# A whole transformer step on one core: FFN tiles from unnormed rows, row broadcasts by diagonals, a moved branch, idle products

## The chip, the core and the metric

The kernel runs on one core of a Trainium2 chip. The metric is device time in microseconds (us) of one execution. TensorE is called PE, VectorE DVE, ScalarE ACT, GpSimd POOL, SyncE SP; SP issues the weight transfers. A *pass* is one matmul of the trace; a row of the order of instructions (below) can stand for several.

## The reference

256 tokens of 1024 numbers go through one block (retention and gated delta rule, then a mixture of 32 experts of which each token takes two) and then through a pooling mixer and a convolutional FFN. What the change touches is this:

```python
    # router: top-1 group, top-2 experts in it; then, over the tokens of each expert,
    hid = silu(xs @ w1[e]) * (xs @ w3[e]);  ys = (hid @ w2[e]) * gate
    x = x + gate2 * ffn
    x = rmsnorm(x, final_norm_w)                       # a row of 1024 weights
    # pooling mixer: x + scale * (pool(rms_norm(x, norm_mix_g)) @ w + b)
    # FFN:
    h = causal_depthwise_conv(rms_norm(x, norm_ffn_g) @ w_in, conv_w, conv_b)   # 1024 -> 5632, 3 taps
    val, gate = split(h, 2)
    out = x + (silu(gate) * val) @ w_out               # 2816 -> 1024
```

## The kernel before, in words

The kernel is one long program without loops on the chip. The front (projections, retention, delta rule) takes until about 232 us, the router until about 240, the experts until 682, the pooling mixer until 708, the FFN until the end.

**Experts.** The loop over `p` (0 to 15) takes two experts each, 64 slots per expert in each half of the 128 rows. For one p PE does w1 and w3 (L1268: 64 passes of 128x512), then ACT the silu (L1273), DVE the product `hid` (L1274), PE the scatter of the pair before (L1226), transposes of `hid` (L1279), at odd p the gather of the tokens of the next two pairs (L1203), then `slot_rows` (L1213, L1215) and w2 (L1291: 32 passes). Six weight blocks of 2 MB per pair come by SP's queue into a ring of slots: a block is asked for when the products that read the slot's old content are done. For p = 15 each block comes in four pieces. At p = 12 `load_tail` closes one part of the ring, leaves six slots, and makes three broadcast rows: it loads 1x3072 numbers by DMA, and six matmuls with a contraction of 1 (L1039) spread them over 128 rows.

**Overflow.** An expert with more than 64 tokens is handled by `overflow()` (L1153), a `tc.If` on a count in SBUF. Every engine loads the count (L1154) and branches (L1155). The body is not run for these inputs. The call stands between the first gather and w1 of p = 0.

**Tail.** `pw` is multiplied by the scale row `psb` on POOL (L1334). The statistics of both norms run on ACT and DVE, L1372 is the pooling product, `zs` its evacuation (L1376, L1378), L1388 the banded product, and four adds make the new rows x (L1391, one for each half of the two token tiles t = 0, 1). Then come squares (L1392), root and reciprocal (L1394 to L1396), the scaled rows `v` (L1399), their transposes (L1414), and two parts of each transposed row block: the rounded `gh` (ACT, L1419) and the rest `gl` (DVE, L1422).

**FFN.** `up(j)` (j = 0 to 10) makes four products of 24 passes (L288: three parts, eight blocks each). Before a product its weights are split into `wh` (ACT, L279) and `wl` (DVE or POOL, L282). After it ACT applies the last tap (L1443) and DVE two shifted taps (L1446, `yf`), then silu (L1449), a product on POOL (L1450) and a split into `hfh` and `hfl`. Four PSUM banks take turns.

Inside the experts the order of PE and SP is that of the code (`tc.manual_schedule`), in the router that of DVE. A scheduler orders the rest.

Of the kernel before, what the change touches and what calls it, by code (L numbers as in the profile page):

```python
# [9 lines left out]
F32 = mybir.dt.float32  # L10
F32R = mybir.dt.float32r
# [8 lines left out]
D = 1024  # L20
# [39 lines left out]
def _consts():  # L60
# [38 lines left out]
    def pack(d):  # L99
        off, cols, n = {}, [], 0  # L100
        for k, v in d.items():
# [10 lines left out]
         ("bge", 40), ("fnT", 8), ("mixgT", 8), ("ffngT", 8), ("fconvw", 132), ("fconvb", 44)]  # L112
# [8 lines left out]
def layout(inp):  # L121
# [56 lines left out]
def build(ctx, tc, io, out, dbg=None):  # L178
# [842 lines left out]
    def load_tail():  # L1021
        ringd.close()
        rings["c"] = ctx.enter_context(tc.tile_pool(name="ringc", bufs=RING_C, reuse_waits="tile"))
        slots[:] = [s for s in slots if s[0] in "efh"] + [["c", None] for i in range(RING_C)]
        tail_w["split"] = ctx.enter_context(tc.tile_pool(name="ffnw", bufs=1, reuse_waits="tile"))
        tlw = tlws.enter_context(tc.tile_pool(name="tailw", bufs=1, reuse_waits="tile"))

        def tw(shape, name):
            return tlw.tile(shape, F32, name=name)

        cp = tw([128, CP.shape[1]], "cp")
        pw = tw([128, 4, 2, 256], "pw")
        rows = tw([128, 3, D], "rows")
        rf = rows.rearrange("p i d -> p (i d)")
# [7 lines left out]
        tail_w.update(cp=cp, pw=pw, fwb=fwb, pbb=rows[:, 1, :], psb=psb)  # L1042
# [17 lines left out]
    hand.enter_context(tc.manual_schedule(engines={ENG.DVE}))  # L1060
# [49 lines left out]
    V.tensor_tensor(M, oh[0], oh[1], op=ALU.add)  # L1110
    psk = bank("pa")
# [41 lines left out]
    def overflow():  # L1153
            nmax = nc.values_load(bigi[0:1, 0:1], min_val=0, max_val=T)  # L1154
            with tc.If(nmax > SLOTS):  # L1155
# [13 lines left out]
                with tc.For_i(0, NE, 1) as e:  # L1169
                    gcol = sr([128, 2], "gcol")  # L1170
                    V.tensor_copy(gcol, gov[:, :, bass.ds(e, 1)].rearrange("p t o -> p (t o)"))
                    for f in range(4):
                        hps = [bank(), bank()]
                        for i, nm in enumerate(("w1", "w3")):
                            for k4 in range(0, 8, 4):
                                wb = mt([128, 4, 128], "wb", tag="hid")
# [67 lines left out]
    overflow()  # L1244
    for p in range(NE // 2):
# [18 lines left out]
        for nm in ("w1", "w3"):  # L1264
# [117 lines left out]
    w0 = wload(io["ffn_w_in"][0], 8, 512)  # L1382
    for t in range(2):
        for hf in range(2):
# [7 lines left out]
            S.activation(junk, x1[:, t, cs], AF.Square, accum_out=s5[:, t, hf:hf + 1])  # L1392
        r5 = s5[:, t, 1:2]
        V.tensor_scalar(s5[:, t, 0:1], s5[:, t, 0:1], 1.0 / D, EPS, op0=ALU.mult, op1=ALU.add)  # L1394
        S.activation(r5, r5, AF.Sqrt, scale=1.0 / D, bias=s5[:, t, 0:1])
        V.reciprocal(r5, r5)  # L1396
        for hf in range(2):
            cs = slice(512 * hf, 512 * hf + 512)
            V.tensor_scalar(v3[:, t, cs], x1[:, t, cs], r5, None, op0=ALU.mult)  # L1399
    dump("x4", x1)  # L1400
    for i in range(2):
        for vg in range(2):
            c = 256 * vg + 128 * i
            pre.append(split(tail_w["split"], w0[:, :, c:c + 128], [128, 8, 128], "w", NSPLIT))

    gh, gl = [], []
# [3 lines left out]
    for k2 in range(4):  # L1410
        ps = bank("pa").rearrange("p (k t) -> p k t", k=2)
        for t in range(2):
            for k in range(2):
                PE.transpose(ps[:, k, 128 * t:128 * t + 128], v3[:, t, 128 * (2 * k2 + k):128 * (2 * k2 + k) + 128], ident)  # L1414
        h = ff.tile([128, 2, T], F32R, name="gh", tag="gh", bufs=4)
        l = ff.tile([128, 2, T], F32R, name="gl", tag="gl", bufs=4)
        for k in range(2):
            g = ffng[:, 2 * k2 + k:2 * k2 + k + 1]
            S.activation(h[:, k, :], ps[:, k, :], AF.Copy, scale=g)  # L1419
        for k in range(2):  # L1420
            g = ffng[:, 2 * k2 + k:2 * k2 + k + 1]
            V.scalar_tensor_tensor(l[:, k, :], ps[:, k, :], g, h.bitcast(F32)[:, k, :], op0=ALU.mult, op1=ALU.subtract)  # L1422
            gh.append(h[:, k, :])
            gl.append(l[:, k, :])
# [6 lines left out]
    def up(j):  # L1431
        w = wload(io["ffn_w_in"][j], 8, 512) if j else None
        for i in range(2):
            ys = []
            for vg in range(2):
                m = 22 * vg + 2 * j + i
                c = 256 * vg + 128 * i
                wh, wl = split(tail_w["split"], w[:, :, c:c + 128], [128, 8, 128], "w", NSPLIT) if j else pre.pop(0)
                ps = bank()
                for k in range(8):  # L1440
                    mm3(ps[:, :T], wh[:, k, :], wl[:, k, :], gh[k], gl[k], k == 0, k == 7)
                y = ff.tile([128, T], F32, name="yf", tag="yf", bufs=4)
                S.activation(y, ps[:, :T], AF.Identity, scale=cw[:, 3 * m + 2:3 * m + 3], bias=cb[:, m:m + 1])  # L1443
                for tap in range(2):
                    sh = 2 - tap
                    V.scalar_tensor_tensor(y[:, sh:], ps[:, :T - sh], cw[:, 3 * m + tap:3 * m + tap + 1], y[:, sh:],  # L1446
                                           op0=ALU.mult, op1=ALU.add)
                ys.append(y)
            S.activation(ys[1], ys[1], AF.Silu)  # L1449
            G.tensor_tensor(ys[0], ys[0], ys[1], op=ALU.mult)  # L1450
            hid_parts[2 * j + i] = split(ff, ys[0], [128, T], "hf", 8)
# [39 lines left out]
```

## Time and profile before

| | |
|---|---|
| three runs | 893.80, 897.24, 897.35 us; median 897.24 |
| profiled execution | 895.82 us; span 894.0 us, mean granted clock 0.978 |
| busy PE / DVE / ACT / POOL | 843.3 / 387.0 / 271.0 / 147.0 us |
| DMA | 288.52 MB, mean 323 GB/s over the span |
| L1268 and L1291 on PE | 229.0 and 115.4 us |
| L288 on PE | the three FFN forms 97.9, 97.7 and 97.7 us |

PE is busy for 94% of the span, so time can only go where PE waits, or where it does work that can be left out. From 280 to 710 us the DMA engines are full as well. A row of a timeline gives the start, the length, the engine and the line; "[2.12 <-DVEq L1155]" says that the engine had been idle for 2.12 us, and what let it go on. "PEldq", "ACTq" are the engines' sequencers.

### The profile page before, as it was taken

The page shows a single profiled execution, that of the slowest core. Times are in us where ns is not written, and L with a number is a line of the kernel's source. Part 1 is how long each engine was busy: PE and PEld are TensorE (multiplying, and loading weights), DVE is VectorE, ACT ScalarE, POOL GpSimd, SP SyncE. Part 2 cuts the span into 40 slices and gives each one's busy share as a digit, 9 for nine tenths or more (in the row PEclk, how much of TensorE's full clock was granted, in tenths as well). Part 3 has the DMA queues.
Part 4 walks back from the last instruction along what each step waited for, and adds up shares of the span by engine and source line. Part 5 has one row for each costly group of instructions (what it writes and reads, how often), then busy time and mean ns, then how long its engine had stood idle before and what let it go on. Part 6 is the DMA issues. An engine that isn't in the chain of part 4 may idle for free.

```text
span 894.0 us, 12890 instructions
## 1 busy us (share of the span) xinstructions
PE 843.3 (94%) x5326; PEld 532.7 (60%) x5326; DVE 387.0 (43%) x708; ACT 271.0 (30%) x505; POOL 147.0 (16%) x107
## 2 busy tenths in 40 slices
PE   3988999989889999999999998999998899999998
PEld 0665788767733434343343433434434799999996
DVE  2477587586511222221122211322115776566564
ACT  2244144364410101010010100201003575555652
POOL 0244331162000000000000000000002024523525
PEclk9899999999999999999999999899999999999999
DMA  9982679767579999999999999999999935454001
GB/s 372 423 358 98 284 263 378 290 254 321 189 264 403 427 427 428 427 427 427 427 426 427 429 427 427 427 385 429 421 409 425 426 122 221 154 229 186 1 2 47
DMA packets 26112, 288.52 MB, mean 323 GB/s; under 512 B 3009, under 2 KB 3393, under 8 KB 9793
## 3 DMA queue, kind: packets, MB, share of 16 engines
q1 hardware_dynamic: 26050, 287.66, 78.3%
q8 instruction: 43, 0.70, 0.3%
q14 instruction: 19, 0.16, 0.0%
HBM read 286.60 MB, written 1.05 MB: 322 GB/s over the span
## 4 chain that ended last, share of the span: by engine, by line
PE 59%; DMA 9%; DVE 2%; issue 1%; ACT 1%; SPq 0%; ACTq 0%
PE ps L288 20%; PE ps L1268 19%; PE ps L1291 11%; DMA wt<-in_w 9%; PE ps L1226 3%; PE ps L1203 3%; PE ps L1279 1%; PE ps L1039 1%; PE ps L1215 1%; DVE wl L282 0%; PE ps L1213 0%; DVE x L1474 0%; DVE x L1391 0%; PE ps L1362 0%; ACT gh L1419 0%
## 5 line engine op out<-in xcount | busy, mean ns | idle before, releaser
L1268 PE MATMUL ps<-wt,x 128*64 128x512 f32 x1024 | 229.0, 600 | 5.4 <-DMA wt<-in_w 3.2
L1268 PEld LDWEIGHTS ps<-wt,x 128*64 128x64 f32 x1024 | 76.2, 138 | 150.8 <-issue 137.8
L279 ACT ACTIVATE wh<-wt 128x512 fp32r<-128x512 f32 (+1 forms) x138 | 114.1, 833 | 92.8 <-PE ps L288 84.4
L1291 PE MATMUL ps<-wt,hidT 128*64 128x512 f32 x512 | 115.4, 599 | 2.7 <-issue 1.9
L282 POOL TENSOR_TENSOR wl<-wt,wh 128x512 fp32r<-128x512 f32 (+1 forms) x52 | 96.0, 1857 | 86.6 <-ACT wh L279 84.1
L282 DVE TENSOR_TENSOR wl<-wt,wh 128x1024 fp32r<-128x1024 f32 (+1 forms) x86 | 84.0, 986 | 43.0 <-ACT wh L279 42.5
L1274 DVE SCALAR_TENSOR_TENSOR hid<-ps,gs,hid 128x512 f32<-128x512 f32 x16 | 12.0, 750 | 203.6 <-PE ps L1268 203.6
L288 PE MATMUL ps<-gh,wh 128*128 128x256 f32 x352 | 97.9, 279 | 1.4 <-ACT gh L1419 1.4
L288 PE MATMUL ps<-gl,wh 128*128 128x256 f32 x352 | 97.7, 278 | 0.0
L288 PE MATMUL ps<-gh,wl 128*128 128x256 f32 x352 | 97.7, 278 | 0.0
L1334 POOL TENSOR_TENSOR pw<-pw,rows 128x512 f32<-128x512 f32 x4 | 5.0, 1270 | 467.5 <-DVE Yf L1298 467.5
L1291 PEld LDWEIGHTS ps<-wt,hidT 128*64 128x64 f32 x512 | 39.2, 138 | 65.7 <-issue 63.0
L288 PEld LDWEIGHTS ps<-gh,wh 128*128 128x128 f32 x352 | 66.7, 190 | 1.8 <-ACT gh L1419 1.6
L288 PEld LDWEIGHTS ps<-gl,wh 128*128 128x128 f32 x352 | 66.8, 190 | 0.2
L288 PEld LDWEIGHTS ps<-gh,wl 128*128 128x128 f32 x352 | 66.7, 189 | 0.0
L1302 ACT ACTIVATE Yh<-ps 128x512 fp32r<-128x512 f32 x30 | 17.9, 597 | 108.3 <-DVE ps L1300 63.6
L1446 DVE SCALAR_TENSOR_TENSOR yf<-ps,sm,yf 128x254 f32<-128x254 f32 x88 | 41.7, 479 | 12.3 <-ACT yf L1443 10.8
L1300 DVE TENSOR_TENSOR ps<-ps,g2b 128x512 f32<-128x512 f32 x30 | 21.0, 699 | 59.9 <-PE ps L1291 59.9
L1273 ACT ACTIVATE hid<-ps 128x512 f32<-128x512 f32 x16 | 9.6, 597 | 110.3 <-PE ps L1268 110.3
L215 ACT ACTIVATE x<-ps,modT,A 128x256 f32<-128x256 f32 x32 | 17.8, 565 | 77.4 <-PE ps L1203 77.4
L1450 POOL TENSOR_TENSOR yf<-yf 128x256 f32<-128x256 f32 x22 | 19.7, 894 | 99.3 <-ACT yf L1449 66.0
L380 PE MATMUL ps<-wt,srep 128*32 128x512 f32 x160 | 24.5, 751 | 11.8 <-DMA wt<-in_w_ada 11.8
(376 smaller groups left out, 1253.1 us busy)
## 6 DMA issues: line engine op xcount, KB each, us to landing
wt<-in_w SPq DMA_DIRECT2D x86, 2048.0 KB, 21.6
wt<-in_w_ada SPq DMA_DIRECT2D x12, 2048.0 KB, 14.0
wt<-in_ffn_w_in SPq DMA_DIRECT2D x11, 2048.0 KB, 12.2
wt<-in_w SPq DMA_DIRECT2D x40, 512.0 KB, 10.2
wt<-in_w_in SPq DMA_DIRECT2D x7, 2048.0 KB, 14.1
wt<-in_ffn_w_out SPq DMA_DIRECT2D x5, 2048.0 KB, 7.6
wt<-in_w_out SPq DMA_DIRECT2D x2, 2048.0 KB, 8.1
wt<-in_w_in SPq DMA_DIRECT2D x2, 1024.0 KB, 19.5
```

Of the source, the lines that this page charges most:

```text
L279: S.activation(hi, src, AF.Copy)
L282: (eng or V).tensor_tensor(lo, src, hi.bitcast(F32), op=ALU.subtract)
L288: PE.matmul(ps, lhsT=a, rhs=b, start=first and n == 0, stop=last and n == 2)
L380: PE.matmul(ps[32 * q:32 * q + 32, :], lhsT=srep[:, 2 * q + kk, :], rhs=w[:, 2 * q + kk, :], start=kk == 0, stop=kk == 1)
L1203: PE.matmul(ps[d - d % 2][:, d % 2, :], lhsT=x[:, t, 128 * d:128 * d + 128], rhs=OH[:, t].rearrange("p g s -> p (g s)"), start=t == d % 2 ...
L1226: PE.matmul(res[t, c], lhsT=oT[:, 128 * t:128 * t + 128], rhs=y, start=False, stop=False)
L1268: PE.matmul(ps[64 * g:64 * g + 64, :], lhsT=xg[:, k, 128 * (p % 2) + 64 * g:128 * (p % 2) + 64 * g + 64], rhs=wt[p, nm, g][:, k, :], start ...
L1291: PE.matmul(py[c][64 * g:64 * g + 64, :], lhsT=hidT[:, f, 64 * g:64 * g + 64], rhs=wt[p, "w2", g][:, f, 512 * c:512 * c + 512], start=f == ...
L1300: V.tensor_tensor(py[c], py[c], g2c, op=ALU.mult)
L1302: S.activation(yh, py[c], AF.Copy)
L1446: V.scalar_tensor_tensor(y[:, sh:], ps[:, :T - sh], cw[:, 3 * m + tap:3 * m + tap + 1], y[:, sh:], op0=ALU.mult, op1=ALU.add)
L1450: G.tensor_tensor(ys[0], ys[0], ys[1], op=ALU.mult)
```

## The change

There are five edits.

1. `spin()` puts five 128x128 matmuls into the router, whose results nobody reads: three before the ranks, two after the counts. PE's order in the router is now that of the code.
2. `overflow()` is called behind the w1 products of p = 0. The silu follows w1 at once for every p.
3. The three broadcast rows are made at p = 13, behind the scatter: POOL makes diagonals (128x512, two buffers), and PE multiplies them with a matrix of ones over the full contraction. The row DMA is gone.
4. `pw` is no longer scaled; `zs` takes the scale row in its evacuation, all four on DVE. The transposed rows of t = 1 are evacuated by ACT in eight pieces.
5. The FFN starts with the unscaled rows x: tiles j = 0, 1 use `gh0` and `gl0` from x, and DVE multiplies the eight products in PSUM by the row of reciprocal norms `r5`. `norm_row()` makes `r5` after the second product. The scaled rows `v`, their 16 transposes and `gh`, `gl` for j of 2 and more are made during j = 1.

```diff
+    def spin(n):
+        ps = bank("pa")
+        for i in range(n):
+            PE.matmul(ps[:, :128], lhsT=ident, rhs=ident, start=True, stop=True)
...
-        nc.sync.dma_start(rf[0:1, :], io["rows"])
-        V.tensor_tensor(rows[0:1, 1, :], rows[0:1, 1, :], rows[0:1, 2, :], op=ALU.mult)
-        for i in range(6):
-            ps = bank("pa")
-            PE.matmul(ps, lhsT=cav("ones")[0:1, :], rhs=rf[0:1, 512 * i:512 * i + 512], start=True, stop=True)
-            copy(rf[:, 512 * i:512 * i + 512], ps)
...
+    def tail_rows():
+        bp = tail_w["pool"].tile([128, 8], F32, name="bp", tag="bp")
+        V.tensor_tensor(bp, smv("pbT"), smv("psT"), op=ALU.mult)
+        for i, col in enumerate((smv("fnT"), bp, smv("psT"))):
+            for hf in range(2):
+                dg = tail_w["pool"].tile([128, 4, 128], F32, name="dg", tag="dg", bufs=2)
+                G.tensor_tensor(dg, ident[:, None, :].to_broadcast([128, 4, 128]),
+                                col[:, 4 * hf:4 * hf + 4, None].to_broadcast([128, 4, 128]), op=ALU.mult)
+                ps = bank("pa")
+                PE.matmul(ps, lhsT=cav("ones"), rhs=dg.rearrange("p b c -> p (b c)"), start=True, stop=True)
+                copy(tail_w["rows"][:, i, 512 * hf:512 * hf + 512], ps)
...
     gather(0, OH)
-    overflow()
     for p in range(NE // 2):
...
+            if nm == "w1":
+                hid = mt([128, DE], "hid")
+                S.activation(hid, ps, AF.Silu)
+                if not p:
+                    overflow()
...
         if p:
             scatter(*prev, 1)
+        if p == 13:
+            tail_rows()
...
-    for g in range(4):
-        G.tensor_tensor(pw[:, g], pw[:, g], psb[:, None, 256 * g:256 * g + 256].to_broadcast([128, 2, 256]), op=ALU.mult)
...
+            V.scalar_tensor_tensor(zs[:, t, cs], ps, s4[:, t, 1:2], psb[:, cs], op0=ALU.mult, op1=ALU.mult)
...
+    rows_T(x1, gh0, gl0)
...
+    def norm_row():
+        psr = bank("pa")
         for t in range(2):
+            for hf in range(2):
+                S.activation(junk, x1[:, t, 512 * hf:512 * hf + 512], AF.Square, accum_out=s5[:, t, hf:hf + 1])
...
+            V.tensor_scalar(dg, ident, r, None, op0=ALU.mult)
+            PE.matmul(psr[:, 128 * t:128 * t + 128], lhsT=cav("ones"), rhs=dg, start=True, stop=True)
+            V.tensor_scalar(v3[:, t], x1[:, t], r, None, op0=ALU.mult)
+        S.activation(r5, psr[:, :T], AF.Copy)
...
+        ahead = [product(*m) for m in tiles[:0 if j else 2]]
+        if not j:
+            norm_row()
...
+            if j < 2:
+                V.tensor_tensor(ps[:, :T], ps[:, :T], r5, op=ALU.mult)
...
+            if i and j == 1:
+                rows_T(v3, gh, gl, (2 * vg, 2 * vg + 1))
```

PE at the start of the experts, before (`xh`, `xl`: rows of all tokens; `wt`: a weight block; the body of the branch is left out):

```order
L1203 MATMUL ps<-OH,xh 128x256 x16
L1203 MATMUL ps<-OH,xl 128x256 x16
L1154 TENSOR_LOAD router
L1155 COMPARE_AND_BRANCH
...
L1155 UNCONDITIONAL_BRANCH x2
L1268 MATMUL ps<-wt,x_73 64x512 x32
```

and after, where lines have moved by 14 or 15 numbers:

```order
L1083 MATMUL ps<-ca 128x128 x2
L1218 MATMUL ps<-OH,xh 128x256 x16
L1218 MATMUL ps<-OH,xl 128x256 x16
L1282 MATMUL ps<-wt,x_73 64x512 x16
L1169 TENSOR_LOAD router
L1170 COMPARE_AND_BRANCH
...
L1170 UNCONDITIONAL_BRANCH x2
L1282 MATMUL ps<-wt,x_73 64x512 x16
```

Half of the 32 rows (the w1 products) now stands ahead of the branch, the w3 half behind it, and two idle products ahead of the gather.

PE at the broadcast rows, before, behind the scatter of p = 11 and ahead of w1 of p = 12:

```order
L1226 MATMUL ps<-Yh,oT 128x512
L1226 MATMUL ps<-Yl,oT 128x512
L1039 MATMUL ps<-rows,ca 128x512 x6
L1268 MATMUL ps<-wt,x_73 64x512 x32
L1226 MATMUL ps<-Yh,oT 128x512
```

and after, at p = 13, ahead of the transposes of `hid`:

```order
L1282 MATMUL ps<-wt,x_73 64x512 x32
L1241 MATMUL ps<-Yh,oT 128x512
L1241 MATMUL ps<-Yl,oT 128x512
L1241 MATMUL ps<-Yh,oT 128x512
L1241 MATMUL ps<-Yl,oT 128x512
L1048 MATMUL ps<-dg,ca 128x512 x6
L1298 MATMUL ps<-ca,hid 128x128 x4
```

The six matmuls have moved from ahead of a pair's products to the middle of a later pair, and wait there for POOL.

DVE at the start of the FFN, before, from the `gl` parts on:

```order
L1422 SCALAR_TENSOR_TENSOR gl<-ps,sm,gh 128x256 x8
L282 TENSOR_TENSOR wl<-wt,wh 128x1024
L1446 SCALAR_TENSOR_TENSOR yf<-ps,sm,yf 128x254
L1446 SCALAR_TENSOR_TENSOR yf<-ps,sm,yf 128x255
L282 TENSOR_TENSOR wl<-wt,wh 128x1024
```

and after, at the end of tile j = 1:

```order
L283 TENSOR_TENSOR wl<-wt,wh 128x1024
L1493 SCALAR_TENSOR_TENSOR yf<-ps,sm,yf 128x254
L1435 SCALAR_TENSOR_TENSOR gl<-ps,sm,gh 128x256
L283 TENSOR_TENSOR hfl<-yf,hfh 128x256
L1493 SCALAR_TENSOR_TENSOR yf<-ps,sm,yf 128x255
L1435 SCALAR_TENSOR_TENSOR gl<-ps,sm,gh 128x256 x3
L1488 TENSOR_TENSOR ps<-ps,r_4876 128x256
L283 TENSOR_TENSOR wl<-wt,wh 128x1024
L1493 SCALAR_TENSOR_TENSOR yf<-ps,sm,yf 128x254
L1435 SCALAR_TENSOR_TENSOR gl<-ps,sm,gh 128x256
L1493 SCALAR_TENSOR_TENSOR yf<-ps,sm,yf 128x255
L1435 SCALAR_TENSOR_TENSOR gl<-ps,sm,gh 128x256 x3
```

Between the arrival of `r5` and the last of these rows DVE has 8 multiplications by `r5` (L1488), 16 `yf`, 8 `gl`, 3 `hfl` and 8 `wl` (of which two stand ahead of the first L1488).

## Rows read from the trace of the kernel before

**Rows 1.** Windows: stretch, busy us (instructions), PEclk, DMA share, GB/s.

```profile
570.00:580.00 10.00, 10.00 (x23) 3.38 (x24) 2.68 (x4) 2.38 (x4) 0.00 (x0) 0.74 1.00 426
580.00:590.00 10.00, 10.00 (x46) 3.17 (x44) 0.00 (x0) 0.60 (x1) 0.00 (x0) 0.92 0.83 326
```

**Rows 2.** Chain of waits in time order, 560 to 690 us.

```profile
630.33 0.30 SPq L314
```

**Rows 3.** Timeline of PE: start, length, line, operation [idle before <-releaser].

```profile
548.94 7.08 PE L1268 MATMUL ps<-wt,x 128*64 128x512 f32 x30 [2.70 <-DMA wt<-in_w]
...
570.07 5.96 PE L1039 MATMUL ps<-rows,ca 1*128 1x512 f32 x12
575.97 16.75 PE L1268 MATMUL ps<-wt,x 128*64 128x512 f32 x64
...
595.15 7.09 PE L1291 MATMUL ps<-wt,hidT 128*64 128x512 f32 x32 [0.27 <-issue]
...
603.31 13.95 PE L1268 MATMUL ps<-wt,x 128*64 128x512 f32 x64
...
631.34 14.53 PE L1268 MATMUL ps<-wt,x 128*64 128x512 f32 x64
...
648.26 7.43 PE L1291 MATMUL ps<-wt,hidT 128*64 128x512 f32 x32 [0.27 <-issue]
...
656.75 15.10 PE L1268 MATMUL ps<-wt,x 128*64 128x512 f32 x64
...
674.20 7.87 PE L1291 MATMUL ps<-wt,hidT 128*64 128x512 f32 x32 [0.79 <-DVE hidT L206]
```

**Rows 4.** Sequencer rows of the branch, L1154 and L1155: ns min/median/max, first and last start.

```profile
L1154 PEldq TENSOR_LOAD <-router x1: 489/489/489, 242.6 to 242.6; - x1
...
L1155 PEldq COMPARE_BRANCH  x1: 3787/3787/3787, 243.2 to 243.2; - x1
L1155 ACTq COMPARE_BRANCH  x1: 50/50/50, 245.9 to 245.9; - x1
```

**Rows 5.** Timeline of PE around the branch.

```profile
242.97 2.39 PE L1203 MATMUL ps<-OH,xl 128*128 128x256 f32 x16
247.48 2.80 PE L1268 MATMUL ps<-wt,x 128*64 128x512 f32 x12 [2.12 <-DVEq L1155]
```

**Rows 6.** Groups by shape: busy us, mean ns | idle before.

```profile
L1300 DVE TENSOR_TENSOR ps<-ps,g2b 128x512 f32<-128x512 f32 x30 | 21.0, 699 | 59.9 <-PE ps L1291 59.9
...
L356 POOL TENSOR_TENSOR acc<-ca,sm 128x512 f32<-128x512 f32 x4 | 4.2, 1040 | 21.1 <-PE ps L406 21.1
```

**Rows 7.** Timeline of the tail and of PE in the FFN.

```profile
702.48 0.87 DVE L1399 TENSOR_SCALAR v<-x,s 128x512 f32<-128x512 f32 x2
...
703.27 0.68 DVE L1391 TENSOR_TENSOR x<-x,ps 128x512 f32<-128x512 f32 x1
...
705.87 1.09 PE L1414 MATMUL ps<-ca,v 128*128 128x128 f32 x8 [1.70 <-DVE v L1399]
...
707.34 3.23 DVE L1422 SCALAR_TENSOR_TENSOR gl<-ps,sm,gh 128x256 fp32r<-128x256 f32 x8 [1.13 <-ACT gh L1419]
...
708.36 0.55 PE L288 MATMUL ps<-gh,wh 128*128 128x256 f32 x1 [1.40 <-ACT gh L1419]
...
711.27 0.32 PE L288 MATMUL ps<-gl,wh 128*128 128x256 f32 x1
...
734.22 0.28 PE L288 MATMUL ps<-gh,wl 128*128 128x256 f32 x1
```

**Rows 8.** Timeline of DVE in the FFN.

```profile
733.06 0.42 DVE L282 TENSOR_TENSOR hfl<-yf,hfh 128x256 fp32r<-128x256 f32 x1 [1.08 <-ACT hfh L279]
733.40 0.99 DVE L1446 SCALAR_TENSOR_TENSOR yf<-ps,sm,yf 128x254 f32<-128x254 f32 x2
734.31 1.22 DVE L282 TENSOR_TENSOR wl<-wt,wh 128x1024 fp32r<-128x1024 f32 x1
735.45 0.99 DVE L1446 SCALAR_TENSOR_TENSOR yf<-ps,sm,yf 128x254 f32<-128x254 f32 x2
```

More of the change, by code (lines that the diff above doesn't have):

```diff
@@ L1059, in build @@
     hand = ExitStack()
-    hand.enter_context(tc.manual_schedule(engines={ENG.DVE}))
+    hand.enter_context(tc.manual_schedule(engines={ENG.DVE, ENG.PE}))
     scratch, used = mt([128, 512], "router", tag="Yl"), [0]
@@ L1110, in build @@
     V.tensor_tensor(M, oh[0], oh[1], op=ALU.add)
+    spin(3)
     psk = bank("pa")
@@ L1184, in overflow @@
                             cs = slice(512 * c, 512 * c + 512)
-                            w2b = mt([128, 512], "wb", tag="hid")
+                            w2b = mt([128, 512], "wb", tag="Yl")
                             nc.sync.dma_start(w2b, io["w2"][bass.ds(e, 1), :, f, cs].rearrange("o p n -> (o p) n"))
@@ L1343, in stats @@
             PE.transpose(ps[:, d, :], v3[:, t, 512 * c + 128 * d:512 * c + 128 * d + 128], ident)
-        V.tensor_tensor(xT[:, 4 * c:4 * c + 4, tc_], ps, mf[:, 4 * c:4 * c + 4, None].to_broadcast([128, 4, 128]),
-                        op=ALU.mult)
+        if t:
+            for d in range(4):
+                S.activation(xT[:, 4 * c + d, tc_], ps[:, d, :], AF.Copy, scale=mf[:, 4 * c + d:4 * c + d + 1])
+        else:
+            V.tensor_tensor(xT[:, 4 * c:4 * c + 4, tc_], ps, mf[:, 4 * c:4 * c + 4, None].to_broadcast([128, 4, 128]),
+                            op=ALU.mult)
         if c and t:
@@ L1382, in build, with pre_split @@
     w0 = wload(io["ffn_w_in"][0], 8, 512)
+    def pre_split(i, vg):
+        c = 256 * vg + 128 * i
+        pre.append(split(tail_w["split"], w0[:, :, c:c + 128], [128, 8, 128], "w", NSPLIT))
+    pre_split(0, 0)
     for t in range(2):
@@ L1391, in build @@
             V.tensor_tensor(x1[:, t, cs], x1[:, t, cs], ps, op=ALU.add)
[L1392 to L1399, printed above, removed]
-    dump("x4", x1)
[L1401 to L1406, printed above, removed]
+    dump("x4", x1)
     tlws.close()
@@ L1409, in build, with rows_T @@
     ff = ffp.enter_context(tc.tile_pool(name="ffn", bufs=1, side="right", reuse_waits="tile"))
-    for k2 in range(4):
-        ps = bank("pa").rearrange("p (k t) -> p k t", k=2)
-        for t in range(2):
[L1413 to L1424, printed above, removed]
+    def rows_T(x, hi, lo, ks=range(4)):
+        for k2 in ks:
+            ps = bank("pa").rearrange("p (k t) -> p k t", k=2)
+            for t in range(2):
+                for k in range(2):
+                    PE.transpose(ps[:, k, 128 * t:128 * t + 128], x[:, t, 128 * (2 * k2 + k):128 * (2 * k2 + k) + 128], ident)
+            for k in range(2):
+                kk = 2 * k2 + k
+                S.activation(hi[:, kk, :], ps[:, k, :], AF.Copy, scale=ffng[:, kk:kk + 1])
+            for k in range(2):
+                kk = 2 * k2 + k
+                V.scalar_tensor_tensor(lo[:, kk, :], ps[:, k, :], ffng[:, kk:kk + 1], hi.bitcast(F32)[:, kk, :],
+                                       op0=ALU.mult, op1=ALU.subtract)
@@ new lines, in build @@
+    gh, gl = (ff.tile([128, 8, T], F32R, name="g" + c, tag="g" + c) for c in "hl")
+    gh0, gl0 = tt([128, 8, T], "gh0", tag="dT", dtype=F32R), tt([128, 8, T], "gl0", tag="zs", dtype=F32R)
+    rows_T(x1, gh0, gl0)
+    for i, vg in ((0, 1), (1, 0), (1, 1)):
+        pre_split(i, vg)
+    r5 = ff.tile([128, T], F32, name="r5", tag="r5")
+    def norm_row():
+        psr = bank("pa")
+        for t in range(2):
+            for hf in range(2):
+                S.activation(junk, x1[:, t, 512 * hf:512 * hf + 512], AF.Square, accum_out=s5[:, t, hf:hf + 1])
+            r = s5[:, t, 1:2]
+            V.tensor_scalar(s5[:, t, 0:1], s5[:, t, 0:1], 1.0 / D, EPS, op0=ALU.mult, op1=ALU.add)
+            S.activation(r, r, AF.Sqrt, scale=1.0 / D, bias=s5[:, t, 0:1])
+            V.reciprocal(r, r)
+            dg = ff.tile([128, 128], F32, name="dg", tag="dg", bufs=2)
+            V.tensor_scalar(dg, ident, r, None, op0=ALU.mult)
+            PE.matmul(psr[:, 128 * t:128 * t + 128], lhsT=cav("ones"), rhs=dg, start=True, stop=True)
+            V.tensor_scalar(v3[:, t], x1[:, t], r, None, op0=ALU.mult)
+        S.activation(r5, psr[:, :T], AF.Copy)
@@ L1432, in up, with product @@
         w = wload(io["ffn_w_in"][j], 8, 512) if j else None
[L1433 to L1451, printed above, removed]
+        def product(i, vg):
+            c = 256 * vg + 128 * i
+            wh, wl = split(tail_w["split"], w[:, :, c:c + 128], [128, 8, 128], "w", NSPLIT) if j else pre.pop(0)
+            ps = bank()
+            for k in range(8):
+                h, l = (gh, gl) if j > 1 else (gh0, gl0)
+                mm3(ps[:, :T], wh[:, k, :], wl[:, k, :], h[:, k, :], l[:, k, :], k == 0, k == 7)
+            return ps
@@ new lines, in up @@
+        tiles = [(i, vg) for i in range(2) for vg in range(2)]
+        ahead = [product(*m) for m in tiles[:0 if j else 2]]
+        if not j:
+            norm_row()
+        ys = []
+        for i, vg in tiles:
+            m = 22 * vg + 2 * j + i
+            ps = ahead.pop(0) if ahead else product(i, vg)
+            if j < 2:
+                V.tensor_tensor(ps[:, :T], ps[:, :T], r5, op=ALU.mult)
+            y = ff.tile([128, T], F32, name="yf", tag="yf", bufs=4)
+            S.activation(y, ps[:, :T], AF.Identity, scale=cw[:, 3 * m + 2:3 * m + 3], bias=cb[:, m:m + 1])
+            for tap in range(2):
+                sh = 2 - tap
+                V.scalar_tensor_tensor(y[:, sh:], ps[:, :T - sh], cw[:, 3 * m + tap:3 * m + tap + 1], y[:, sh:],
+                                       op0=ALU.mult, op1=ALU.add)
+            ys.append(y)
+            if i and j == 1:
+                rows_T(v3, gh, gl, (2 * vg, 2 * vg + 1))
+            if vg:
+                S.activation(ys[1], ys[1], AF.Silu)
+                G.tensor_tensor(ys[0], ys[0], ys[1], op=ALU.mult)
+                hid_parts[2 * j + i] = split(ff, ys[0], [128, T], "hf", 8)
+                ys = []
```

19 lines of the change are left out of this document (7 added, 12 removed).

## The prediction

> **What bounds the kernel now.** I read the table of busy times first: PE works 843.3 of 894.0 us, so an edit pays only where PE waits or where work leaves PE. The windows come next, for the weights. The DMA engines run at 426 GB/s in 570 to 580 us, as in most of the expert stage, and drop to 326 in the next ten [rows 1]. That hole is (1 - 326/426) x 10 = 2.4 us long. Then the timeline of PE: the w3 products of p = 11 wait 2.70 us for weights, the broadcast matmuls of L1039 take 5.96 us, and the products behind them 16.75 us against 13.95 us one pair later [rows 3]. So L1039 costs 5.96 and another 2.80 for a clock that falls to its lower level on the 1-row matmuls and behind them (0.74 granted in 570 to 580 [rows 1]), 8.8 us of PE. From p = 14 on PE waits for the stream again, in small pieces: 14.53 and 15.10 against 13.95 us in L1268, 7.43 and 7.87 against 7.09 us in L1291, together 0.58 + 0.34 + 1.15 + 0.78 = 2.85 us [rows 3]. The reader should see that the expert stage has two limits, PE and the stream, that take turns: what is taken from the one is partly found again at the other. From 708.36 us on the FFN has PE without a gap [rows 7]; DVE there has little to spare, 1.08 idle of 4.4 us in [rows 8].
>
> **Idle products.** Five short matmuls in the router. Three stand among logit and residual matmuls while the DVE chain runs, two between the counts and the gather. [...] Its second half takes 2.39 us [rows 5] and waits for DVE's rows as well, so that I allow the whole edit a quarter of that at most: bounds 0 and -0.6, taken -0.3.
>
> **The branch.** Before, PE's first w1 pass starts at 247.48 after an idle 2.12 us [rows 5]; the gather ends at 242.97 + 2.39 = 245.36. Behind the gather, w1 can start then: -2.1. But PE now loads the count and branches between w1 and w3, with x us in the open. Before, the load (0.49) began at 242.6, when the gather's matmuls were still being worked off, and the branch then took 3.79 us, against 0.05 on ACT [rows 4]. If PE's sequencer runs that far ahead again, the pair lies under 7 us of w1 products and x is 0; if it must wait for them to end, x is 0.49 + 3.79 and a wake-up, 4.4. ACT reaches its branch behind a table load and the silu, and DVE's `hid` comes behind its own branch, both beside w3. I take x = 1.5, nearer to the hidden case since the load did run ahead in the row. The sum of this edit is -0.6, bounds -2.1 and +2.3.
>
> [...]
>
> **The broadcast rows.** At p = 12, 8.8 us of PE go, but the stream doesn't let PE use them: p = 12 and 13 need weights that land at most 2.4 us earlier (the hole goes, since the slots it waited for come free earlier) plus what the start gained, 0.6 + 0.3. So the products of p = 13 end 3.3 us earlier, not 9. Then the new step: six diagonals on POOL and twelve passes on PE. A POOL operation of this shape takes 1.04 us [rows 6]; the twelve passes took 5.96 us at L1039, partly at the low clock [rows 3], and an eighth less, 5.2, at the high one. With two buffers the first two diagonals are ready ahead, and the other four take turns with the matmuls that free their buffers (0.9 us a pair of passes): the last matmul ends 5.9 us after the first starts, with handovers 6.3. Bounds: 5.2 (POOL never waited for) and 6 x 1.04 + 0.98 = 7.2 (all six in a row). PE has nothing else to do in that time: the transposes of `hid` and all that follows stand behind the six matmuls. Next, w2 of p = 13 ends 6.3 - 3.3 = 3.0 us later than before, and SP's request for the next slots, at 630.33 right behind it [rows 2], is as much later; the stream has a new hole of some 1.3 us, less than it gained. PE then does p = 14 and 15 without the 2.85 us of waits. Experts: -3.3 + 6.3 - 2.85 = +0.2, with the first two edits in it. With their bounds and those of the step: -2.4 - 2.1 - 0.6 + 5.2 - 2.85 = -2.8, and -2.4 + 2.3 + 7.2 - 2.85 = +4.3.
>
> **The scale row.** POOL's 5.0 us at L1334 and two ACT evacuations go; DVE takes four of 0.7 us, and ACT eight short copies. The pooling product waits for the transposed rows and not for `pw`, so this is 0, and at worst 0.7, one evacuation ahead of the banded product, which the next edit's 0.65 covers.
>
> **The start of the FFN.** Without the scaled rows between the adds (0.87 us at 702.48, right before the last add at 703.27 [rows 7]) the last add ends at about 703.3 and not 703.95. The transposes follow at once, and the first product starts at about 704.0 and not 708.36. That is -4.4. PE has to do more: 16 transposes, 1.09 us for eight [rows 7], and two matmuls for `r5`, +2.5. If nothing else were short, the edit would bring -1.9.
>
> DVE is short. It can't go beyond the two first splits until `r5` is there: 704.0 and 48 passes at 0.1135 (202 passes from 711.27 to 734.22 [rows 7]), the first 13 at 0.22 where the clock is low as now (708.36 to 711.27), then two matmuls, a copy and three handovers, 1.6: 711.1 to 712.5, taken 712.0. From there to the last `gl`, which the ninth product needs, the order holds 7 splits at 1.14 (one of the eight is done by then), 16 taps at 0.455 and 3 `hfl` at 0.34 (distances between starts in [rows 8]), 8 `gl` at 3.23/8 = 0.40 [rows 7], and 8 multiplications by `r5`. The trace has no such multiplication; one of twice the width takes 0.70 [rows 6], so half is 0.35, I take 0.37 (bounds 0.33 and 0.45). Sum: 8.0 + 7.3 + 1.0 + 3.2 + 3.0 = 22.5. DVE also waits, in my replay of its order, 1.3 us for PE and ACT. So the last `gl` is there at 735.8, the ninth product ends 0.34 later at 736.1, against 734.22 + 0.11 = 734.3 before: +1.8. PE waits about 2 us each at the eighth and ninth product, for a bank and for `gl`. With the lengths of [rows 8] in place of the distances (1.23, 0.50, 0.42), 0.45 for the new operation and the late `r5` it is +4.3; the other end is -1.9. From the tenth product on nothing is given back, since PE has no gaps to fill.
>
> **The sum.** -0.3 - 0.6 + 1.1 (rows, so that the experts are +0.2) + 1.8 = +2.0. On the profiled execution, 895.82 (its span and 1.8 us around it), that is 897.8; it lies 1.4 below the median of 897.24, and by the median the sum is 899.2. I give the middle, 898.5. What a measurement can tell from no change is 0.5%, 4.5 us: "same" is 892.8 to 901.7.
>
> **The rivals.**
> - *DVE keeps up and the branch is hidden (faster).* For it: PE's sequencer ran ahead in [rows 4], and DVE is idle for a quarter of the stretch in [rows 8]. Against it: DVE's list is 22.5 us long where PE's eight products take 21.8. With both, -2.8 - 1.9 = -4.7: 891.1 on the profile, 892.5 on the median, 891.8.
> - *Handovers in DVE's fixed order (slower).* Each of the first eight products now goes DVE, ACT, DVE (multiply, first tap, two taps) with other work in between in a fixed order. If a split stands ahead of a tap that is ready, or the other way round, DVE idles as it does in [rows 8] ahead of `hfl`, 1.08 us. With 0.75 per product this is 6 us and not 1.3: +4.7 on the forecast, 903.2. It decides from about 0.7 us of waiting per product on; the rows of before, with waits of 0.5 to 1 us in most products, speak for it, that DVE had slack there which filled them against it.
> - *The branch in the open (slower or same).* x = 4.4 gives +2.9 on the forecast, 901.4. Its place is the gap between the w1 and the w3 products of p = 0. For it: 3.79 us on PE; against it: the load at 242.6.
> - *The broadcast move doesn't do what it says.* For the most part this is in the forecast: of 8.8 us of PE only 2.4 arrive at p = 13. Even if the new step cost nothing, the experts would end 3.3 us earlier and not 8.8, since the stream would end them: 895.0, still no measurable change. It has no chance of its own.
>
> **Chances.** The forecast 0.42, handovers 0.17, the open branch 0.16, the faster case 0.25. Of the forecast's own spread (895 to 902) a twentieth each falls outside of "same"; of the open branch about half is slower. Faster 0.25 + 0.02 = 0.27, slower 0.17 + 0.08 + 0.03 = 0.28, same 0.45. The range runs from the faster case, 891.5, to just beyond the handovers, 904.5.
>
> **What would show it.** The first w1 pass at 245.4 and a gap of 0 to 4.4 us ahead of w3; no hole in the stream at 580 to 590 and one near 634; PE waiting for POOL's diagonals for about 1 us in the p = 13 step; the first FFN product at 704 with the eighth and ninth waiting on DVE. It is wrong if PE doesn't wait for weights at p = 12 and 13, or if the ninth product ends before 734.

## The result: 904.07 us, 0.7% slower, and the profile after

| | before | after |
|---|---|---|
| median of 14 runs each | 897.12 us | 904.07 us |
| lowest and highest | 893.40, 903.91 us | 899.12, 905.14 us |
| profiled execution; span; mean granted clock | 895.82; 894.0; 0.978 | 904.65; 902.9; 0.982 |

The ratio of times is 1.0066 [1.0042, 1.0091], so the change costs 3.8 to 8.2 us. The forecast, no measurable change (892.8 to 901.7), did not hold. That the time still lies inside the predicted range is luck: the upper end of the range was set by a rival that didn't come true. I cut both profiled executions at the same instructions of PE (us; differences of starts read from its timeline):

| stretch | before | after |
|---|---|---|
| up to the gather of p = 0 | 239.8 | 241.6 |
| gather | 5.54 | 5.56 |
| from its end to w2 of p = 0 | 20.37 | 19.10 |
| from its end to the end of the experts | 436.65 | 436.74 |
| tail, up to the first FFN product | 26.35 | 22.09 |
| first nine FFN products | 25.98 | 30.81 |
| from the tenth product to the last pass | 155.90 | 162.16 |

The first row is a chance of that execution: the order of PE is the same up to the router, and the eleven later profiles have 238.8 to 241.9 there, whatever the version. The five edits act in the next five rows, and there they nearly cancel: +0.02, +0.09 for the experts with the branch in them, -4.26, +4.83. The +0.09 is one pair of executions, and the stretch isn't steady: in e2 and e6 (below), whose experts are those of the kernel before, it took 433.2 and 440.2 us, where before has 436.65. The loss stands in the last row, +6.26 us, where nothing was edited.

What fills that row is seen on the two pages of the profile, first before, then after (line, engine, operation, count | busy us, mean ns of one | idle before):

```profile
L288 PE MATMUL ps<-gh,wh 128*128 128x256 f32 x352 | 97.9, 279 | 1.4 <-ACT gh L1419 1.4
```

```profile
PE 853.6 (95%) x5356; PEld 539.3 (60%) x5356; DVE 390.9 (43%) x724; ACT 275.2 (30%) x520; POOL 147.8 (16%) x109
...
L289 PE MATMUL ps<-gh,wh 128*128 128x256 f32 x352 | 99.3, 283 | 2.1 <-DVE yf L1493 1.4
```

The idle time of the three forms of these passes is 1.3 us more, at the first nine products; behind them PE doesn't wait, its passes are longer. The timeline of PE in the middle of the FFN, before, shows it at the starts:

```profile
799.77 0.28 PE L288 MATMUL ps<-gh,wl 128*128 128x256 f32 x1
799.88 0.28 PE L288 MATMUL ps<-gh,wh 128*128 128x256 f32 x1
800.00 0.28 PE L288 MATMUL ps<-gl,wh 128*128 128x256 f32 x1
800.11 0.28 PE L288 MATMUL ps<-gh,wl 128*128 128x256 f32 x1
800.22 0.28 PE L288 MATMUL ps<-gh,wh 128*128 128x256 f32 x1
```

and after:

```profile
799.72 0.28 PE L289 MATMUL ps<-gh,wl 128*128 128x256 f32 x1
799.84 0.28 PE L289 MATMUL ps<-gh,wh 128*128 128x256 f32 x1
799.96 0.28 PE L289 MATMUL ps<-gl,wh 128*128 128x256 f32 x1
800.08 0.28 PE L289 MATMUL ps<-gh,wl 128*128 128x256 f32 x1
800.20 0.28 PE L289 MATMUL ps<-gh,wh 128*128 128x256 f32 x1
```

From the first start to the fifth it is 0.45 us before and 0.48 after, at a granted clock of 1.00 (790 to 810 us) in both. Over whole products of 24 passes the mean distance is 113.0 to 114.8 ns before, and 118.3 to 120.0 after, the one in some groups of products and the other in others (starts are given to 0.01 us, so these means are good to about 0.4 ns). With 840 such passes in the last row, 6.1 ns each are 5.1 us; the 264 passes of 128x512 of the second FFN matrix went from 228.9 to 232.7 ns, another 1.0. Together 6.1 of 6.26.

**What the edits did.** The end of the gather and the branch, after (timeline of PE):

```profile
244.69 2.47 PE L1218 MATMUL ps<-OH,xl 128*128 128x256 f32 x16
247.09 7.09 PE L1282 MATMUL ps<-wt,x 128*64 128x512 f32 x32
255.30 7.09 PE L1282 MATMUL ps<-wt,x 128*64 128x512 f32 x32 [1.12 <-ACTq L1170]
```

and the sequencers at it (ns min/median/max, first and last start):

```profile
L1169 PEldq TENSOR_LOAD <-router x1: 486/486/486, 249.7 to 249.7; - x1
L1169 ACTq TENSOR_LOAD <-router x1: 465/465/465, 254.3 to 254.3; - x1
...
L1170 PEldq COMPARE_BRANCH  x1: 4031/4031/4031, 250.3 to 250.3; - x1
...
L1170 ACTq COMPARE_BRANCH  x1: 50/50/50, 254.8 to 254.8; - x1
```

The gap of 2.12 us [rows 5] ahead of w1 is gone. PE's branch still takes 4.03 us, against 3.79 [rows 4], but from 250.3 to 254.4, nearly all of it under the w1 products, which end at 254.2. What is left in the open, 1.12 us, ends with ACT, which reaches its own branch last.

The step of the broadcast rows at p = 13, after (PE; the scatter and gather rows left out):

```profile
596.97 7.09 PE L1282 MATMUL ps<-wt,x 128*64 128x512 f32 x32 [0.49 <-DMA wt<-in_w]
606.73 8.78 PE L1282 MATMUL ps<-wt,x 128*64 128x512 f32 x30 [2.67 <-DMA wt<-in_w]
...
616.46 1.88 PE L1048 MATMUL ps<-dg,ca 128*128 128x512 f32 x4
618.66 2.12 PE L1048 MATMUL ps<-dg,ca 128*128 128x512 f32 x4 [0.32 <-POOL dg L1045]
620.96 2.12 PE L1048 MATMUL ps<-dg,ca 128*128 128x512 f32 x4 [0.18 <-POOL dg L1045]
622.92 0.60 PE L1298 MATMUL ps<-ca,hid 128*128 128x128 f32 x4
...
627.84 7.09 PE L1310 MATMUL ps<-wt,hidT 128*64 128x512 f32 x32
```

PE waits 0.49 and 2.67 us for the weights of p = 13 and then does the rows, 6.46 us, with nothing else to do. In windows of 10 us (layout as in [rows 1]) the hole in the weight stream has moved to behind that step:

```profile
580.00:590.00 10.00, 9.73 (x48) 5.01 (x46) 2.44 (x5) 0.39 (x1) 0.00 (x0) 1.00 1.01 433
...
630.00:640.00 10.00, 10.00 (x48) 3.57 (x46) 2.78 (x4) 1.19 (x2) 0.00 (x0) 1.00 0.75 290
```

At the FFN's start (PE) the first product, the eighth and the end of the ninth wait for DVE:

```profile
705.99 0.36 PE L289 MATMUL ps<-gh,wh 128*128 128x256 f32 x1 [0.62 <-DVE gl L1435]
...
728.84 0.36 PE L289 MATMUL ps<-gh,wh 128*128 128x256 f32 x1 [1.41 <-DVE yf L1493]
...
735.41 0.39 PE L289 MATMUL ps<-gl,wh 128*128 128x256 f32 x1 [0.58 <-DVE gl L1435]
```

### The profile page after: what moved, and what is told of

Same layout as the page of the kernel before. It is cut to its first block, busy times and chain, and to the rows that moved or that the text cites. A ratio compares the mean times of both kernels' runs of the same rounds, so it can differ in the third digit from the quotient of the medians.

```text
span 902.9 us, 12985 instructions
## 1 busy us (share of the span) xinstructions
PE 853.6 (95%) x5356; PEld 539.3 (60%) x5356; DVE 390.9 (43%) x724; ACT 275.2 (30%) x520; POOL 147.8 (16%) x109
## 4 chain that ended last, share of the span: by engine, by line
PE 62%; DMA 6%; DVE 2%; ACT 1%; issue 1%; POOL 0%; SPq 0%; ACTq 0%
PE ps L1282 22%; PE ps L289 19%; PE ps L1310 11%; DMA wt<-in_w 6%; PE ps L1241 3%; PE ps L1218 3%; PE ps L1298 1%; PE ps L1393 1%; PE ps L1412 1%; PE ps L1230 1%; PE ps L1048 0%; DVE yf L1493 0%; PE ps L1383 0%; PE ps L1228 0%; ACT wh L280 0%
## 5 line engine op out<-in xcount | busy, mean ns | idle before, releaser
L1282 PEld LDWEIGHTS ps<-wt,x 128*64 128x64 f32 x1024 | 72.8, 137 | 153.3 <-issue 139.2
L1045 POOL TENSOR_TENSOR dg<-ca,sm 128x512 f32<-128x512 f32 x4 | 4.1, 1041 | 311.5 <-PE ps L1282 311.3
L381 PE MATMUL ps<-wt,srep 128*32 128x512 f32 x160 | 26.7, 810 | 11.0 <-DMA wt<-in_w_ada 11.0
```

What stands on the lines that cost most here:

```text
L381: PE.matmul(ps[32 * q:32 * q + 32, :], lhsT=srep[:, 2 * q + kk, :], rhs=w[:, 2 * q + kk, :], start=kk == 0, stop=kk == 1)
L1282: PE.matmul(ps[64 * g:64 * g + 64, :], lhsT=xg[:, k, 128 * (p % 2) + 64 * g:128 * (p % 2) + 64 * g + 64], rhs=wt[p, nm, g][:, k, :], start ...
```

## The experiments

What could make passes of unchanged shape longer? Beside the edits that its list names, the change adds two columns of 8 numbers (`pbT`, `psT`) to the small table, which stays in SBUF throughout. In the memory layout of the built program, all split weights `wh`, `wl` stand 64 bytes higher for it (116928 before, 116992 after, in each partition), while the moving rows `gh`, `gl` kept their start modulo 256. The address theory (A): the distance of the two starts sets the length of a pass. The rivals lay it to the other edits. Below, d is (start of the moving rows - start of the weights) modulo 256; it is 192 before, and 128 after for j of 2 and more (224 for j = 0 and 1, which read other tiles).

**e1, after with 64 bytes more.** 16 unread columns at the end of the table.

```diff
-         ... ("fconvw", 132), ("fconvb", 44)]
+         ... ("fconvw", 132), ("fconvb", 44), ("pad", 16)]
```

> The kernel after, with 16 unread columns behind the small table, so that all FFN weight parts (wh, wl) lie 64 bytes higher in each row: 64 past a multiple of 128, as in the kernel before; gh, gl and hfh stay on multiples of 128. Theory A (the distance between two passes depends on whether the moving rows and the stationary block lie in the same 64-byte half of a 128-byte line): the passes of 128x256 go back from 0.120 to 0.1135-0.114 us, those of 128x512 from 0.2325 to 0.229, together 6.5 to 7.5 us less: about 897. Theory B (the layout of gh and gl in one tile, or the order of the products, makes the passes longer): 0.120 stays, 904. Theory C (it was that one execution): times unchanged, and the passes differ from profile to profile.

903.3 us, ratio 1.0054 [1.0032, 1.0075]; passes of 117.4 to 117.8 ns for j of 2 and more (d = 64). The address does change the passes, but 128 bytes from the old place the old length is not back. My first form of A, that only the half of 128 bytes counts, fell.

**e2, before with 64 bytes more.** The same 16 columns, in the kernel before; no other edit.

> The kernel before, with the same 16 unread columns: wh and wl on multiples of 128, as in the kernel after, and gh, gl, hfh on multiples of 128 as ever. Nothing else differs. Theory A: the passes of 128x256 go from 0.114 to 0.120 us (1056 of them, +6.2) and those of 128x512 from 0.229 to 0.2325 (264, +0.9): about 904. Theories B and C: unchanged, 897.

902.13 us, 1.0043 [1.0023, 1.0063]; passes of 118.3 to 120.0 ns (d = 128), and 162.05 us from the tenth product on, as after (162.16). One line of its page, where before has 97.9 us and 279 ns:

```profile
L289 PE MATMUL ps<-gh,wh 128*128 128x256 f32 x352 | 100.5, 286 | 1.4 <-ACT gh L1420 1.4
```

Sixteen columns that nobody reads make the kernel before as slow there as the changed one; the rivals are out.

**e3, the moving rows 64 bytes lower.** The weights stay as after.

```diff
     gh, gl = (ff.tile([128, 8, T], F32R, name="g" + c, tag="g" + c) for c in "hl")
+    G.memset(ff.tile([128, 16], F32, name="pad", tag="pad"), 0.0)
```

> The kernel after, with 16 unread columns behind gh and gl, so that these two lie 64 bytes lower (64 past a multiple of 128), while wh, wl and hfh stay on multiples of 128. Theory A, which looks at the two addresses together: the passes of 128x256 of the tiles j = 2 and later 0.114, those of 128x512 stay at 0.2325; about 898. If only the place of the weights counts: 0.120 and 0.2325, 904.

900.84 us in one run; 117.4 to 117.8 ns for j of 2 and more (d = 64), as in e1, where the other operand had moved. The 128x512 passes, whose rows didn't move, take 233.4 ns, much as after (232.7). That speaks for the distance and against the place of one operand.

**e4, both (e1 and e3).**

> The kernel after with both shifts: wh, wl and gh, gl all 64 past a multiple of 128, hfh on multiples of 128. Theory A: 0.120 for the passes of 128x256 of j = 2 and later (same half again), 0.229 for those of 128x512 (different halves); about 903. If only the place of the weights counts: 0.114 for both tiles' passes, 897.

904.48 us in one run; 118.7 to 120.0 ns (d = 0). The 128x512 passes take 231 and 236 ns in turn, 233.4 in the mean, where I had expected 229: a miss.

**e5, after with 192 bytes more.** 48 columns in place of 16: with the change's own 64 the weights stand 256 above before.

> The kernel after with 48 unread columns behind the small table: wh and wl lie 192 bytes higher. Theory A2 (formed from the first four runs): the distance of two passes depends on d, the start of the moving rows less the start of the stationary block, modulo 256 bytes: 113.3 ns at d = 192 (the kernel before), 117.7 at 64, 118.5 to 120 at 128, 120 at 0. Here d is 192 for the tiles j = 2 and later: 113.3 ns in 36 products, 36 x 24 x 6 ns = 5.2 us less than the kernel after, about 898.5, the ratio to before within 0.3% of 1. Theory B2 (one tile of eight blocks costs 117.7 whatever the place; only the rest is the address): 117.7, 902. The products of j = 0 and 1 have d = 32, for which no run has a number.

898.97 against 898.84 us, 1.0005 [0.9984, 1.0025]; 113.0 to 114.8 ns for j of 2 and more, 156.02 us from the tenth product on (before: 155.90). The timeline of PE has the old steps again:

```profile
799.73 0.28 PE L290 MATMUL ps<-gl,wh 128*128 128x256 f32 x1
799.84 0.28 PE L290 MATMUL ps<-gh,wl 128*128 128x256 f32 x1
799.95 0.28 PE L290 MATMUL ps<-gh,wh 128*128 128x256 f32 x1
800.07 0.28 PE L290 MATMUL ps<-gl,wh 128*128 128x256 f32 x1
800.18 0.28 PE L290 MATMUL ps<-gh,wl 128*128 128x256 f32 x1
```

The whole change with the weights back in place is worth nothing measurable. The loss was the 64 bytes.

**e6, before with 192 bytes more.**

> The kernel before with the same 48 columns: d goes from 192 to 128 - here 0 modulo 256 by 192 - 192. Theory A2: 120 ns in all 44 products, some 7 us more than before. If what counts is only whether the two lie in the same 64-byte half (d modulo 128), then d = 0 is slow as well, 118.5 to 120, and this run does not tell the two apart, but a pass of 113.3 would end both.

907.88 us in one run; 119.7 to 120.0 ns from the third product on (d = 0), 160.91 us from the tenth on. The 128x512 passes are shorter than before, 227.2 ns. Its end of the experts was late as well, 440.18 us behind the gather: the products of p = 11 took 20.2 us where before has 18.4, and L1039 with the products behind it 24.4 where before has 22.7. Both lie ahead of the FFN.

**e7, e5 with the rows ahead of p = 13's products.** There PE had waited 0.49 and 2.67 us for weights.

```diff
+        if p == 13:
+            tail_rows()
         ph = []
...
             scatter(*prev, 1)
-        if p == 13:
-            tail_rows()
```

> The kernel of the run with 48 columns, with the six row matmuls ahead of the products of p = 13 rather than behind its scatter. In the kernel after PE waits 0.49 + 2.67 us for weights in those products and then spends 6.46 us on the rows. If the weight stream sets the time there, the rows fit into the wait and more, p = 13 ends some 6 us earlier and p = 14, 15 wait for the stream as before: the experts end 2.5 to 3.3 us earlier, 895.5. If PE sets it, nothing is gained: 898.5.

894.77 against 898.84 us, 0.9954 [0.9931, 0.9978]. PE's timeline:

```profile
597.26 1.88 PE L1049 MATMUL ps<-dg,ca 128*128 128x512 f32 x4
599.46 2.12 PE L1049 MATMUL ps<-dg,ca 128*128 128x512 f32 x4 [0.32 <-POOL dg L1046]
601.76 2.12 PE L1049 MATMUL ps<-dg,ca 128*128 128x512 f32 x4 [0.18 <-POOL dg L1046]
603.81 13.95 PE L1285 MATMUL ps<-wt,x 128*64 128x512 f32 x64
```

The rows cost the same, but the products of p = 13 now follow without a wait, and the stream has no hole behind them:

```profile
630.00:640.00 10.00, 10.00 (x46) 3.47 (x44) 1.39 (x2) 1.19 (x2) 0.00 (x0) 1.00 1.00 423
```

The experts end 433.27 us behind the gather, 436.23 in e5. Over all profiles of kernels that have the diagonals, it is 431.4 to 433.8 with the rows ahead (e7, e9, e10, e11) and 436.2 to 439.9 with them behind (after, e1, e3, e4, e5, e8).

One thing in this profile doesn't fit. The first three products of j = 2 have d = 192 by the layout, as in e5, yet their passes take 117.8 ns at a granted clock of 1.00 (735 to 741 us):

```profile
739.09 0.28 PE L290 MATMUL ps<-gh,wl 128*128 128x256 f32 x1
739.21 0.28 PE L290 MATMUL ps<-gh,wh 128*128 128x256 f32 x1
739.32 0.28 PE L290 MATMUL ps<-gl,wh 128*128 128x256 f32 x1
739.44 0.28 PE L290 MATMUL ps<-gh,wl 128*128 128x256 f32 x1
```

The 128x512 passes right behind them take 233, and from 754 us on the lengths are those of e5 again. So the distance alone doesn't fix the length.

**e8, e5 with the branch in its old place** (`overflow()` behind the gather).

> The kernel of the run with 48 columns, with the overflow branch ahead of the first w1 products again. By the trace of after the move brought 2.17 us at the start of w1 and cost 1.12 us between w1 and w3: so w2 of p = 0 starts 1.0 us later here, counted from the end of the gather. If the branch in the open cost nothing, 2.1; if it cost all, 0.

901.23 us in one run. The wait ahead of w1 is back, and w2 of p = 0 starts 20.41 us behind the gather and not 19.31: the moved branch is worth 1.1 us.

```profile
247.55 12.67 PE L1284 MATMUL ps<-wt,x 128*64 128x512 f32 x58 [2.57 <-PEq L1171]
```

The experts ended 3.7 us later than in e5, more than I had expected: 1.1 is the branch, 1.7 is w2 of p = 0 (0.83 granted in 260 to 270), whose length varies from 7.1 to 9.4 us over the profiles, and most of the rest lies in the products of p = 13, 19.9 us against 18.5.

**e9, e7 with d = 192 in every product.** Pads in the pools of the split weights and the tail in place of the table's columns, so that `gh0`, `gl0` of j = 0, 1 stand right as well (and one pad in the front).

```diff
+        G.memset(tail_w["split"].tile([128, 48], F32, name="pad0", tag="pad0"), 0.0)
...
+    G.memset(tt([128, 40], "pad1"), 0.0)
...
+    G.memset(tt([128, 24], "pad2"), 0.0)
```

> The kernel of the run with the rows ahead of p = 13, with unread columns placed so that d is 192 for all products of 128x256: FFN tiles j = 0 and 1 (there 32, 116.5 to 118 ns) and the projections of the front (there 0, about 119 ns); the front's and the FFN's 512-column passes get 64 in place of 0 and 64. Theory A2: products 1 to 7 of the FFN at 113.3 ns, 0.7 to 0.9 us less; the 192 passes of 128x256 of the front at 113.3, 1.1 us less, and up to 1.2 in its 312 passes of 128x512, as far as PE is what the front waits for. Together 1 to 3 us: about 892.5. If d did not matter in the front: 894.

891.23 against 898.97 us, 0.9914 [0.9888, 0.994]: the lowest median of all versions. The early FFN products run at 113.0 ns too where PE has their operands; the first nine take 30.35 us, only 0.3 less than in e7, since PE waits 1.78 and 0.61 us for DVE in them. In the front the passes go with d as well. In e7 (d = 0), as in every other profile, most of its 128x256 passes start 120 ns apart; in e9 (d = 192) most start 113 or 114 ns apart. First e7, then e9:

```profile
115.04 0.28 PE L290 MATMUL ps<-hl,wh 128*128 128x256 f32 x1
115.16 0.28 PE L290 MATMUL ps<-hh,wl 128*128 128x256 f32 x1
115.28 0.28 PE L290 MATMUL ps<-hh,wh 128*128 128x256 f32 x1
115.40 0.28 PE L290 MATMUL ps<-hl,wh 128*128 128x256 f32 x1
```

```profile
115.06 0.28 PE L289 MATMUL ps<-hh,wh 128*128 128x256 f32 x1
115.17 0.28 PE L289 MATMUL ps<-hl,wh 128*128 128x256 f32 x1
115.28 0.28 PE L289 MATMUL ps<-hh,wl 128*128 128x256 f32 x1
115.40 0.28 PE L289 MATMUL ps<-hh,wh 128*128 128x256 f32 x1
```

But the front ends no earlier: the gather starts at 239.1, inside the 238.8 to 241.9 of the others. There the miss is in what PE's shorter passes are worth, not in their length. The experts end 431.4 us behind the gather, 1.9 earlier than in e7, for which I have no cause.

**e10, e7 with the normed start of the FFN from before.**

```diff
-    rows_T(x1, gh0, gl0)
...
+            V.tensor_scalar(v3[:, t, cs], x1[:, t, cs], r5, None, op0=ALU.mult)
```

> The kernel of the run with the rows ahead of p = 13, with the FFN head of the kernel before (normed rows from the first tile on, d = 192 for all tiles). By the traces, tail and first nine products take 22.08 + 30.65 = 52.73 us with the unnormed head and 52.33 in the kernel before: 0.4 us less, no measurable difference, 894.4. If the unnormed head were worth the 4.3 us that the tail alone shows: 899.

892.34 us, 0.9932 [0.9903, 0.9962]. Tail and first nine products take 51.59 us; with the unnormed start it is 52.73 in e7, whose early passes are long, and 52.4 in e9, where they are short as here. The unnormed start gains nothing even with the passes short.

**e11, before with the row edit alone,** in e7's place, weights back at d = 192.

> The kernel before with one part of the change, the rows by diagonals, ahead of the products of p = 13, and the FFN weights placed so that d stays 192. Theory (the weight stream sets the experts, and a step laid into PE's wait for it costs nothing): no low clock at p = 12, no hole in the stream, the experts take about 434.4 us from the end of the gather (433.3 in the run with all edits, plus 1.1 for the branch), 2 to 3 us less than before: 895. If the gain of the run with all edits came from elsewhere: 898.

891.43 us, 0.9918 [0.9887, 0.9949]. This one edit, well placed, gives as much as all of them in e9; the intervals of e9, e10 and e11 overlap. It is more than the 2 to 3 us that I had expected: its experts end 433.8 us behind the gather, as forecast to 0.6 us, and what the rest of the gain in the median comes from isn't shown.

Passes of 128x256 in the FFN against the distance of the starts, over all versions, in products that ran at a granted clock of 1.00 without a wait:

| d | ns per pass | seen in |
|---|---|---|
| 192 | 113.0 to 114.8 | before, e5, e7 to e11 |
| 192 | 117.8 | e7, first three products of j = 2 |
| 64 | 117.4 to 117.8 | e1, e3 |
| 128 | 118.3 to 120.0 | after, e2 |
| 0 | 118.7 to 120.0 | e4, e6 |

The products of j = 0 and 1 on unnormed rows have d = 224, 160 or 32 (but for e9) and take 116.7 to 118.9 ns where they don't wait.

## Why the prediction was right or wrong, step by step

- **The step that failed** is "passes at 0.1135" (it priced the FFN's products), and with it "from the tenth product on nothing is given back", which put the last stretch at nothing. I took the passes of the kernel before for those of the kernel after, since shapes and order were the same. They became 6.1 ns longer: +6.26 us from the tenth product on. Two columns in a table did it, which I had counted among no part of the change. No rival had it either, so that the measured time lies in the range by luck.
- **Idle products**: -0.3 forecast, 0.0 measured (5.54 to 5.56 us), and no effect shown over the other runs. That idle products raise the clock in the gather was my guess; no run shows it, nor the 0.3 us. With them the gather took 5.5 to 5.6 us in after, e1, e3, e4, e7 and e10 and 4.64 in e5, e8 and e9; without them 5.5 to 5.6 in before, e2 and e6 and 4.64 in e11. It is the clock that makes the difference (granted 0.70 from 241.6 to 247.2 in after, 1.00 from 239.9 to 244.6 in e5), but it comes out either way whether or not the idle products are there. The high clock is worth 0.9 us, more than the bound of 0.6.
- **The branch**: -0.6 forecast (x = 1.5), -1.3 measured in the profile, -1.1 in e8. The pair on PE lies under w1, as the early load had suggested; x was 1.12 and ended with ACT, which I had put beside w3. So the rival of the open branch, x = 4.4, fell. PE's branch is long in either place, 3.79 us [rows 4] and 4.03, and why isn't shown. While the matmuls ahead of it were still being worked off, 2.2 us of the first ran and 3.9 of the second.
- **The rows**: right in mechanism, and in size for the step. It took 6.46 us, forecast 6.3, with 0.5 us of waiting for POOL, forecast about 1; the hole moved to 630 to 640 us; PE waited for weights ahead of p = 13; the w1 and w3 products of p = 14 and 15 took 13.95 us each, w2 of p = 15 again 0.78 us behind `hidT`. Experts +0.09, forecast +0.2, but a match as close as that is luck in a stretch that varies by 7 us over three executions of the same experts (433.2, 436.65, 440.2). What I had not drawn from my own working is its use: PE waits 3.2 us right ahead of the new step, and e7 puts the step there, for 3.0 us.
- **The start of the FFN**: -4.26 up to the first product, forecast -4.4. The first two multiplications by `r5`, which follow on each other, start 0.33 to 0.34 apart, forecast 0.37. Tail and nine products together +0.57, forecast +1.8. The longer passes of j = 0 and 1 (216 passes of some 5 ns, 1.1 us) explain little of it: with short ones, in e9, the two stretches take 52.4 us, against 52.9 after. The kernel before loses time there to the low clock (0.50 granted from 708.36 to 711.27, 178 ns per pass in its first product; 1.00 granted and 122 ns after); e9 against e10 gives +0.9. So it is DVE-bound as forecast: PE waits for `yf` and `gl`, 1.4 and 0.6 us; the rival in which DVE keeps up is out, and so is that of handovers, which wanted 0.75 us of waiting in each product: PE waits at two of the nine.

Without the step that failed, the sum of the forecast was near: e5, which is that case, measured 1.0005 [0.9984, 1.0025], the forecast +2.0 us or 1.002.

## What to carry to other kernels

When an edit adds or drops a tile that stays in memory, compare the start addresses of all that comes behind it, and the distance of equal passes in the trace, before judging the edit itself: here 64 bytes outweighed five edits. Put work that nothing waits for where the engine waits anyway, and not beside it: the same 6.5 us, moved from behind the products of p = 13 to ahead of them, shortened the experts by 3 us.

## What was unexpected in the hardware

At a granted clock of 1.00 the starts of two 128x256 passes of the FFN's first matrix (L288 before), each with its weight load, stand 113 to 120 ns apart, and which it is goes, but for the three products of e7, with the distance of the starts of the two operands modulo 256: 6%, and 6 us of 900 in this kernel. The runs show the dependence from both operands (e1, e3) and without any other edit (e2, e6). They show the short passes at two places, with the rows at 128 and the weights at 192 modulo 256 in the FFN, and at 160 and 224 in the front of e9.

For the 128x512 passes of the FFN the order is another: 227.2 ns at d = 0 (e6), 228.9 at 64 (before, e5), 232.7 to 233.4 at 128 (after, e2, e3), 233.3 to 233.4 at 192 (e1, e4). The front has 0 and 64 as well: most of its passes take 227 ns at d = 0, and 226, 229 or 232 in e9 at 64.

The reason isn't shown. Nor is what decides where one distance gives two lengths, as d = 128 does (118.3 and 120.0) and d = 192 in e7 (117.8 ahead of 754 us, 113.3 behind it).
